# Attention of a hybrid layer with its scores turned: queries on the partitions instead of keys

## The chip, the cores and the metric

The kernel runs on one NeuronCore of a Trainium2 chip. The metric is device time in microseconds. TensorE multiplies (PE in the rows; PEld is its weight load, which runs beside it), VectorE (DVE), ScalarE (ACT) and GpSimd (POOL) do the element-wise work, and SyncE (SP) issues most transfers. Each engine takes its instructions strictly in the order of the built program; engines meet at semaphores.

## The reference, cut to what matters

One layer of a network over 512 latent tokens and 128 context tokens with 1024 features: modulated norm, one input projection that feeds an mLSTM (4 heads) and a latent attention (8 heads), an output projection over both, a residual, and an MLP. All of it is float32. The part that the change touches is the attention:

```python
def one(qi):
    s = jnp.einsum('bqhd,bkhd->bhqk', qi, kf) * scale
    p = jax.nn.softmax(s, axis=-1)
    return jnp.einsum('bhqk,bkhd->bqhd', p, vf)
```

For each of 8 heads, 512 latent queries attend to 640 keys (512 latent and 128 of the cached context), with 96 features in a query or key and 64 in a value. The 128 context tokens attend to their own 128 keys. The results of both go side by side into the rows 512 to 1023 of the operand of the output projection; the mLSTM's are rows 0 to 511.

## The kernel before

Tokens are kept as columns and features as partitions; a product that must be near float32 is taken as three products of parts: the high part `hi` (a cast to float32r on ScalarE) and the remainder `lo` (source less high part, on VectorE), as `hi*hi + hi*lo + lo*hi`. `split` (L108) makes the two. PSUM has two pools: `psD` has two tiles of two banks, `psS` four tiles of one bank. A helper `two` (L633) gives the 640 columns that lie in the two banks of a `psD` tile as 2 x 320.

The stage in question lies between the projections of queries and keys and the output projection. For each head, `head_q` and `head_k` (L911, L925) transpose the queries (`Tq`) and keys (`Tk`) to feature-major and split them. `row_max` (L934) multiplies the high parts with queries on partitions, four tiles of 640 columns, and takes the row maximum; `max_row` (L943) turns the four columns of maxima into one row, which rides as a 97th row of the contraction. `weights` (L971) takes for each of five blocks of 128 keys the scores with keys on the partitions, 512 query columns (`st`, L975 to L977), then the exponential, which ScalarE writes to SBUF, and its split `pu`; GpSimd adds the five blocks up into `tot` (L997) and makes one of the five remainders. `values` (L1000) multiplies the parts with the values into `pv`, adds the two halves, and writes 64 rows of `mix_a`. `sums` (L1016) takes the column sums of `tot` by products with ones; `normalise` (L1027) spreads the reciprocals of two heads over the partitions (`rdb`) and multiplies `mix_a`. `self_scores` and `self_out` (L950, L962) do the context's own queries (`cs`, `co`).

The loop at L1054 writes these steps in a pipelined order: the values follow the weights by two steps, the next head's preparation stands between the blocks of this one, and the normalisation follows by nine steps. The scheduler of the framework (`schedule_with_timeline_sim=True` at the launch) then chooses the order on each engine itself, from its own estimate of times, and the order in which a pool's tiles come free.

The output projection multiplies eight column blocks of weights by eight inputs: inputs 0 to 3 are the mLSTM's (`mh`, `ml` of `mix_m`), 4 to 7 are pairs of attention heads. `mmT` (L624) issues 6 products of 320 columns for each input. Its first two blocks, `wo0` and `wo4`, sit in both `psD` tiles; their inputs 0 to 3 are taken early, as work beside the last heads, inputs 4 to 7 after the last normalisation:

```python
with tc.issue_after(factors.ins):
    mmT(ps, w_first, MHv, MLv, KT, 4)
```

Then `gated` (L1109) adds the finished tile to the residual on VectorE (`xr`), which starts a long run of VectorE work up to the MLP.

## Time and profile before

| what | us |
|---|---|
| median of 3 runs | 898.63 |
| lowest and highest run | 898.08, 899.42 |
| span of the profiled execution | 896.7 |
| busy in the span: TensorE | 855.5 |
| VectorE | 637.7 |
| ScalarE | 407.6 |
| GpSimd | 341.7 |

The profile is of one execution on the one core; its own time is not listed apart, and its span, first instruction to last, is 1.9 us under the median of the runs. "Busy" counts the time that an engine had at least one instruction in work. TensorE's matmuls overlap and their ends are modelled, so its issue is read from the distance between starts. A row of the order of time has start, duration, engine, line, operation, output and inputs with shapes, and, in brackets, how long the engine was idle before and what released it. A row of a table by stretch has its two ends, its length, and the busy time (number of instructions) of each engine, then the granted TensorE clock as a share of full speed, the share of the transfer engines and GB/s. A row of grouped instructions has line, engine, operation, output and inputs, shapes and count, then the sum of busy time in us and the mean of one in ns, then idle time before them.

### The profile page before, as it was taken

The numbers are of one execution on the slowest core, as the hardware profiler recorded it, in microseconds if no ns is written. First come the engines' busy times: TensorE is split into PE (matmuls) and PEld (weight loads), VectorE is DVE, ScalarE is ACT, GpSimd is POOL, SyncE is SP. The second block draws the span as 40 slices with busy tenths as digits, with TensorE's granted clock in tenths as the row PEclk, the third lists the DMA queues.
The fourth block names the chain that finished last, engine by engine and source line by source line (L and its number), as shares of the span: only waits on it lengthen the run. The fifth ranks groups of instructions, "written<-read, shape, count | busy, mean of one in ns | idle before, by whom it ended". The sixth has DMA issues, their size and how long they took to land.

```text
span 896.7 us, 15205 instructions
## 1 busy us (share of the span) xinstructions
PE 855.5 (95%) x5775; PEld 797.9 (89%) x5775; DVE 637.7 (71%) x1276; ACT 407.6 (45%) x879; POOL 341.7 (38%) x343
## 2 busy tenths in 40 slices
PE   3999999999889999999979999999999999999998
PEld 2688789999768677799979999999999999999998
DVE  3754634546787789969989587695876949678673
ACT  3424426436864688844436143351434415244430
POOL 3100113313234567734745254352534427254320
PEclk9999999999999999999989999999999999999999
DMA  9742843231326100322130312122122221412122
GB/s 356 312 129 69 297 153 90 65 95 51 95 80 249 58 1 1 118 71 88 44 129 25 118 48 95 51 90 96 48 94 92 72 75 48 134 56 71 49 96 92
DMA packets 22329, 89.64 MB, mean 100 GB/s; under 512 B 3144, under 2 KB 3944, under 8 KB 18928
## 3 DMA queue, kind: packets, MB, share of 16 engines
q1 hardware_dynamic: 19440, 81.95, 26.5%
q0 software_dynamic: 1664, 4.26, 1.7%
q10 hardware_dynamic: 1152, 2.46, 0.7%
q8 instruction: 46, 0.75, 0.4%
q14 instruction: 27, 0.22, 0.1%
HBM read 85.33 MB, written 3.32 MB: 99 GB/s over the span
## 4 chain that ended last, share of the span: by engine, by line
PE 74%; DVE 16%; DMA 4%; issue 3%; ACT 3%; POOL 0%; SPq 0%; DVEq 0%; POOLq 0%; ACTq 0%
PE dn L630 23%; PE qk L630 6%; PE mo L630 3%; DMA st<-in_w_ada 3%; DVE wu L110 2%; PE pv L1006 2%; PE ada L389 2%; PE n L695 2%; PE up1M L1228 2%; PE wo L630 2%; DVE r L1272 1%; PE up8M L1228 1%; PE up10M L1228 1%; PE up14M L1228 1%; PE up15M L1228 1%
## 5 line engine op out<-in xcount | busy, mean ns | idle before, releaser
L1266 POOL TENSOR_TENSOR r<-r,rbs 128x320 f32<-128x320 f32 x64 | 77.3, 1222 | 120.7 <-DVE r L1244 118.8
L109 ACT CAST wh<-st 128x1024 fp32r<-128x1024 f32 (+4 forms) x69 | 69.4, 1008 | 105.2 <-PE dn L630 40.3
L1111 DVE SCALAR_TENSOR_TENSOR xr<-dn,modT,xr 128x320 f32<-128x320 f32 x64 | 35.2, 550 | 106.6 <-PE dn L630 106.6
L630 PE MATMUL dn<-fl,wh 128*128 128x320 f32 x448 | 103.6, 310 | 3.0 <-DVE fl L1273 3.0
L630 PE MATMUL dn<-fh,wh 128*128 128x320 f32 x448 | 103.0, 309 | 0.0
L630 PE MATMUL dn<-fh,wl 128*128 128x320 f32 x448 | 101.8, 309 | 0.0
L110 DVE TENSOR_TENSOR wl<-st,wh 128x1024 fp32r<-128x1024 f32 (+4 forms) x67 | 83.3, 1244 | 24.3 <-ACT wh L109 23.3
L109 ACT CAST wu<-S 128x512 fp32r<-128x512 f32 x64 | 37.6, 617 | 105.3 <-issue 46.7
L630 PEld LDWEIGHTS dn<-fl,wh 128*128 128x128 f32 x448 | 75.1, 188 | 4.6 <-DVE fl L1273 4.6
L630 PEld LDWEIGHTS dn<-fh,wh 128*128 128x128 f32 x448 | 75.3, 188 | 0.0
L630 PEld LDWEIGHTS dn<-fh,wl 128*128 128x128 f32 x448 | 74.9, 188 | 0.0
L1270 ACT ACTIVATE r<-r 128x192 f32<-128x192 f32 (+2 forms) x96 | 40.9, 464 | 41.0 <-DVE r L1244 27.3
L110 DVE TENSOR_TENSOR wu<-S,wu 128x512 fp32r<-128x512 f32 x64 | 55.6, 879 | 0.8 <-ACT wu L109 0.8
L722 POOL TENSOR_TENSOR W<-ngb,mask 128x128 f32<-128x128 f32 x40 | 19.3, 498 | 68.9 <-DVE p L732 30.9
L1272 DVE TENSOR_TENSOR r<-r 128x320 f32<-128x320 f32 x64 | 45.0, 721 | 0.2
L997 POOL TENSOR_TENSOR tot<-tot,p 128x512 f32<-128x512 f32 x24 | 37.2, 1549 | 5.9 <-ACT p L979 3.9
L219 POOL TENSOR_TENSOR S<-st,st 128x512 f32<-128x512 f32 x8 | 13.5, 1682 | 59.4 <-DVE wu L110 59.4
L109 ACT CAST wu<-pair 128x512 fp32r<-128x512 f32 x24 | 14.1, 615 | 47.4 <-PE dn L630 41.1
L110 DVE TENSOR_TENSOR pu<-p,pu 128x512 fp32r<-128x512 f32 x32 | 33.2, 1050 | 2.5 <-ACT pu L109 2.5
L1273 DVE TENSOR_TENSOR fl<-r,fh 128x320 fp32r<-128x320 f32 x56 | 32.4, 598 | 0.2
L1006 PE MATMUL pv<-pu,v 128*128 128x512 f32 x80 | 29.1, 426 | 2.3 <-DVE pu L110 2.0
L630 PE MATMUL wo<-mh,wh 128*128 128x320 f32 x128 | 29.6, 311 | 0.7 <-DVE xr L1113 0.7
(485 smaller groups left out, 2420.1 us busy)
## 6 DMA issues: line engine op xcount, KB each, us to landing
st<-in_w_ada SPq DMA_DIRECT2D x16, 1024.0 KB, 5.6
st<-in_w_down SPq DMA_DIRECT2D x32, 512.0 KB, 3.4
ad<-in_w_ada SPq DMA_DIRECT2D x8, 1024.0 KB, 16.7
st<-in_w_up SPq DMA_DIRECT2D x16, 512.0 KB, 3.8
pair<-in_w_up SPq DMA_DIRECT2D x16, 512.0 KB, 4.8
st<-in_w_qko SPq DMA_DIRECT2D x12, 512.0 KB, 3.6
st<-in_w_out SPq DMA_DIRECT2D x8, 512.0 KB, 3.4
x<-in_x SPq DMA_DIRECT2D x4, 640.0 KB, 7.0
```

The costliest lines, as they stand in the source:

```text
L109: S.copy(hi, src)
L110: return eng.tensor_tensor(out=lo, in0=src, in1=f(hi), op=ALU.subtract)
L630: PE.matmul(out[:, hf * 512:hf * 512 + HT], lhsT=wt[:, c], rhs=xt[k][:, hf * HT:(hf + 1) * HT], start=(k == 0 and xt is xh and wt is hi), ...
L722: G.tensor_tensor(out=W[:, dg:dg + P], in0=nb_[dr][:, j * P:(j + 1) * P], in1=mask[:, dr, :], op=ALU.add)
L997: G.tensor_tensor(out=tot[h], in0=first, in1=pj, op=ALU.add)
L1006: PE.matmul(pacc[h], lhsT=v_u[hf][:, j, hh_, :], rhs=w, start=j == 0 and k == 0, stop=j == 4 and k == 1)
L1111: V.scalar_tensor_tensor(out=xr[m][:, 0:HT], in0=ps[:, 0:HT], scalar=modT[:, gi_ + m, 0:1], in1=xr[m][:, 0:HT], op0=ALU.mult, op1=ALU.add)
L1228: PE.matmul(ps, lhsT=w[:, c], rhs=b[k], start=k == 0 and w is hi and b is bh, stop=k == 3 and w is lo)
L1266: G.tensor_tensor(out=t, in0=t, in1=rbs[:, c], op=ALU.mult)
L1270: S.activation(out=t[:, c0:c1], in_=t[:, c0:c1], func=AF.Relu, bias=r[n][:, w:w + 1])
L1272: V.tensor_tensor(out=t, in0=t, in1=t, op=ALU.mult)
L1273: V.tensor_tensor(out=FL[n][:, c], in0=t, in1=f(FH[n][:, c]), op=ALU.subtract)
```

## The change

Scores are now taken with queries on the partitions, all three parts, so that one tile of 128 queries by 640 keys (`sc`) gives its own row maximum; ScalarE's exponential takes that as bias and returns the row sum, VectorE takes its reciprocal, and GpSimd scales the row tile (`prow`, 128 x 640) in place. `turn` transposes the scaled weights on TensorE, a block of 128 keys at a time (`tp`), and splits from PSUM. `row_max`, `max_row`, the ones row, the addition `tot`, `sums` and `normalise` go. `Tq` moves from `psD` to `psS` and leaves the context's queries to `Tk`; two small copies `qc`, `kc` move from ScalarE to VectorE. In the loop the turns of a head follow its scores by five steps and the values by seven; seven of the eight inputs of the output projection are split inside the loop and come before the last wait, one after it. The diff, without the bodies of the functions that are dropped whole (they are above) and without two constants that only these used:

```diff
...
     mix_a = view(mix[1], 0, 4, T)
-    prep, negm, cden, punit, tot, pacc = {}, {}, {}, {}, {}, {}
+    prep, punit, pacc, prow = {}, {}, {}, {}
     def evac(ps, hi, lo, g):
...
         prep[h] += [u[:, 0:P], u[:, P:2 * P]]
-        qh, ql_, kh, kl_, qc, kc = prep[h]
-        G.memset(f(kh)[QK:QK + 1], 1.0)
-        pt = psD(f"Tq{h}")
-        for i in range(NT):
+        qh, ql_ = prep[h][0:2]
+        pt = psS(f"Tq{h}")
+        for i in range(4):
             PE.transpose(out=pt[0:QK, i * P:(i + 1) * P], in_=qn_u[hf][:, i, hh_, :], identity=ident)
         evac(pt[0:QK, 0:TL], qh[0:QK], ql_[0:QK], hgc[:, 0:1])
-        S.activation(out=qc[0:QK], in_=pt[0:QK, TL:T], func=AF.Copy, scale=hgc[:, 0:1])
     def head_k(h):
...
             PE.transpose(out=pt[0:QK, i * P:(i + 1) * P], in_=kn_u[hf][:, i, hh_, :], identity=ident)
+        PE.transpose(out=pt[0:QK, 6 * P:7 * P], in_=qn_u[hf][:, 4, hh_, :], identity=ident)
         evac(pt[0:QK, 0:T], kh[0:QK], kl_[0:QK], hgc[:, 1:2])
-        S.activation(out=kc[0:QK], in_=pt[0:QK, T:T + P], func=AF.Copy, scale=hgc[:, 1:2])
-    def row_max(h, i):
+        V.tensor_scalar(out=kc[0:QK], in0=pt[0:QK, T:T + P], scalar1=hgc[:, 1:2], scalar2=None, op0=ALU.mult)
+        V.tensor_scalar(out=qc[0:QK], in0=pt[0:QK, T + P:T + 2 * P], scalar1=hgc[:, 0:1], scalar2=None, op0=ALU.mult)
+    def soften(out, ps, axis, name):
+        nm, sr = sm("nm", [P, 1], bufs=3), sm("sr", [P, 1], bufs=3)
+        V.tensor_reduce(out=nm, in_=ps, axis=axis, op=ALU.max, negate=True)
+        e = S.activation(out=out, in_=ps, func=AF.Exp, bias=nm, accum_out=sr)
+        V.reciprocal(out=sr, in_=sr)
+        return e, sr
+    def scores(h, i):
         qh, ql_, kh, kl_, qc, kc = prep[h]
         if i == 0:
...
+            prow[h] = view(U2(php, f"p{h}"), 0, 4, T)
+        ps = psD(f"sc{h}{i}")
+        c = slice(i * P, (i + 1) * P)
+        for n_, (l_, r_) in enumerate(((qh, kh), (qh, kl_), (ql_, kh))):
+            for hf in range(2):
+                PE.matmul(ps[:, hf * 512:hf * 512 + HT], lhsT=l_[0:QK, c], rhs=r_[0:QK, hf * HT:(hf + 1) * HT], start=n_ == 0, stop=n_ == 2)
+        p_ = prow[h][:, i, :]
+        e, sr = soften(tw(p_), two(ps), AX.XY, f"{h}{i}")
+        G.tensor_scalar(out=p_, in0=p_, scalar1=sr, scalar2=None, op0=ALU.mult)
+        return e
     def self_scores(h):
...
         PE.matmul(ps, lhsT=qc[0:QK], rhs=kc[0:QK], start=True, stop=True)
...
         pc_ = view(wwp.tile([P, 512], F32, tag="W", name=f"pc{h}"), 0, 2, P)
-        S.activation(out=pc_[:, 0], in_=ps, func=AF.Exp, bias=mx, accum_out=cden[h])
+        e, sr = soften(pc_[:, 0], ps, AX.X, f"{h}c")
+        G.tensor_scalar(out=pc_[:, 0], in0=pc_[:, 0], scalar1=sr, scalar2=None, op0=ALU.mult)
         return pc_
...
         S.copy(mix_a[b:b + VD, h // 2, TL:T], ps[0:VD, P:2 * P])
...
+    def turn(h, j):
+        ps = psS(f"tp{h}{j}")
+        for i in range(4):
+            PE.transpose(out=ps[:, i * P:(i + 1) * P], in_=prow[h][:, i, j * P:(j + 1) * P], identity=ident)
+        if h < AH - 2:
+            pool, tag = ((whp, "wh"), (wlp, "wl"))[(5 * h + j) % 2]
             u = pool.tile([P, 1024], F32R, tag=tag, name=f"pu{h}{j}")
             hi, lo = u[:, 0:TL], u[:, TL:2 * TL]
...
         else:
...
+            hi, lo = (Tt(f"pu{h}{j}{k}", F32R, n=TL) for k in range(2))
+        split(hi, lo, ps)
+        punit[h, j] = hi, lo
     def values(h, j):
...
         for k, w in enumerate((hi, lo)):
-            PE.matmul(pacc[h], lhsT=v_u[hf][:, j, hh_, :], rhs=w, start=j == 0 and k == 0, stop=j == 4 and k == 1)
+            last = PE.matmul(pacc[h], lhsT=v_u[hf][:, j, hh_, :], rhs=w, start=j == 0 and k == 0, stop=j == 4 and k == 1)
         if j == 4:
...
             V.tensor_tensor(out=mix_a[b:b + VD, h // 2, 0:TL], in0=ps[0:VD], in1=tmp, op=ALU.add)
...
         return last
...
     head_k(0)
...
     pcs = {}
     mhu, mlu = [], []
...
+    MSP = ((4, 1), (4, 3), (5, 1), (5, 3), (6, 1), (6, 3), (7, 3))
+    DT, DV = 5, 7
+    for n in range(5 * AH + DV):
+        h, j = divmod(n, 5)
+        if h < AH:
+            if h == AH - 1 and j == 0:
                 wsplit(state["get"] + 3)
-            if (h, j) == (7, 4):
-                w_first = wget(("out", 0))
-                ps_first = psD("wo0")
-                mmT(ps_first, w_first, kview(mhu * 2), kview(mlu * 2), KT, 0, 4)
-            exp_, lo_ = weights(h, j)
+            if j < 4:
+                exp_ = scores(h, j)
             if (h, j) in MSP:
                 k = MSP.index((h, j))
-                if k == 0:
-                    mhu.append(U("mh0", F32R))
-                    mlu.append(U("ml0", F32R))
-                with tc.issue_after(exp_.ins), tc.issue_after(lo_.ins):
-                    split(view(mhu[0], k * T, T), view(mlu[0], k * T, T), mix_m[:, k, :])
...
+                if k % 4 == 0:
+                    mhu.append(U(f"mh{k // 4}", F32R))
+                    mlu.append(U(f"ml{k // 4}", F32R))
+                src = mix_m[:, k, :] if k < MH else mix_a[:, k - MH, :]
+                with tc.issue_after(exp_.ins):
+                    split(view(mhu[k // 4], (k % 4) * T, T), view(mlu[k // 4], (k % 4) * T, T), src)
+            if j == 1 and h + 1 < AH:
+                head_q(h + 1)
+            if j == 2 and h + 1 < AH:
+                head_k(h + 1)
             if j == 3:
+                pcs[h] = self_scores(h)
+            if j == 4:
                 self_out(h, pcs.pop(h))
...
+        if n == 5 * AH:
+            w_first = wget(("out", 0))
+            ps_first = psD("wo0")
+            mmT(ps_first, w_first, kview(mhu), kview(mlu), KT, 0, 7)
+        if 0 <= n - DT < 5 * AH:
+            turn(*divmod(n - DT, 5))
+        if 0 <= n - DV < 5 * AH:
+            factors = values(*divmod(n - DV, 5))
     MHv, MLv = kview(mhu), kview(mlu)
-    for k in range(4, KT):
-        split(MHv[k], MLv[k], mix_a[:, k % 4, :])
+    split(MHv[KT - 1], MLv[KT - 1], mix_a[:, KT - 1 - MH, :])
     xu2 = [U("xr0"), U("xr1")]
...
             with tc.issue_after(factors.ins):
-                mmT(ps, w_first, MHv, MLv, KT, 4)
+                mmT(ps, w_first, MHv, MLv, KT, 7)
         elif m == OUT_ORDER[1]:
...
             w = wnext(("out", m))
-            mmT(ps, w, MHv, MLv, KT, 0, 4)
+            mmT(ps, w, MHv, MLv, KT, 0, 7)
             with tc.issue_after(factors.ins):
-                mmT(ps, w, MHv, MLv, KT, 4)
+                mmT(ps, w, MHv, MLv, KT, 7)
         else:
```

*TensorE, heads 1 to 3.* In the names, the digits are head and block: `sc20` is the first score tile of head 2, `tp10` the first turned block of head 1. Before:

```order
L940 MATMUL mx30_3561<-qk3_3496 128x320 x2
L1020 MATMUL su1_3543<-ones_99,tot1_3392 128x2 x4
L940 MATMUL mx31_3565<-qk3_3496 128x320 x2
L975 MATMUL st22_3550<-qk2_3370 128x512
L976 MATMUL st22_3550<-qk2_3370 128x512
L977 MATMUL st22_3550<-qk2_3370 128x512
L940 MATMUL mx32_3582<-qk3_3496 128x320 x2
L1006 MATMUL pv2_3569<-pu20_3493,v0_2602 128x512
```

After:

```order
L946 MATMUL sc20_3443<-qk2_3342 128x320 x6
L990 MATMUL pv0_3392<-pu02_3389,v0_2598 128x512
L990 MATMUL pv0_3392<-pu03_3422,v0_2598 128x512
L946 MATMUL sc21_3466<-qk2_3342 128x320 x6
L990 MATMUL pv0_3392<-pu03_3422,v0_2598 128x512
L965 MATMUL co1_3427<-ident_94,pc1_3410 128x128
L974 MATMUL tp04_3432<-ident_94,p0_3219 128x128 x4
L974 MATMUL tp10_3456<-ident_94,p1_3307 128x128 x4
L967 MATMUL co1_3427<-pc1_3410,vctx_2596 64x128
L990 MATMUL pv0_3392<-pu04_3437,v0_2598 128x512
L946 MATMUL sc22_3501<-qk2_3342 128x320 x6
```

The scores of head 2 went from single-bank tiles, read by ScalarE alone, to double-bank tiles; the first turn of head 1 stands two score tiles behind that head's last one, and the third score tile of head 2 is behind that turn and behind `co1`.

*ScalarE, at the same place.* Before:

```order
L959 ACTIVATE pc2_3536,cd_3535<-cs2_3531,mx_3533 128x128
L109 CAST pu21_3516<-p21_3514 128x512
L979 ACTIVATE p22_3554<-st22_3550 128x512
L109 CAST pu22_3556<-p22_3554 128x512
L979 ACTIVATE p23_3576<-st23_3572 128x512
L966 COPY pc2_3536<-co2_3590 128x128
L109 CAST pu23_3578<-p23_3576 128x512
L979 ACTIVATE p24_3601<-st24_3597 128x512
```

After:

```order
L934 ACTIVATE p1_3307,sr_3403<-sc13_3395,nm_3402 128x640
L934 ACTIVATE pc1_3410,sr_3412<-cs1_3408,nm_3411 128x128
L966 COPY pc1_3410<-co1_3427 128x128
L109 CAST pu04_3437<-tp04_3432 128x512
L934 ACTIVATE p2_3442,sr_3451<-sc20_3443,nm_3450 128x640
L934 ACTIVATE p2_3442,sr_3474<-sc21_3466,nm_3473 128x640
L109 CAST pu10_3461<-tp10_3456 128x512
```

The exponential of a block was followed by its own cast; now two exponentials of the next head stand behind the copy of `co1`, whose weights GpSimd has scaled.

*TensorE, the end of the stage.* Before:

```order
L1020 MATMUL su7_4296<-ones_99,tot7_4188 128x2 x4
L1038 MATMUL rdb3_4303<-ident_94,rd_4207 64x128
L1038 MATMUL rdc3_4304<-ident_94,rd_4207 64x128 x2
L630 MATMUL wo0_4253<-mh1_4317,wh45_4157 128x320 x2
L630 MATMUL wo0_4253<-ml1_4318,wh45_4157 128x320 x2
L630 MATMUL wo0_4253<-mh1_4317,wl45_4158 128x320 x2
L1006 MATMUL pv7_4220<-pu72_4216,v1_2715 128x512
L630 MATMUL wo0_4253<-mh1_4317,wh45_4157 128x320 x2
L630 MATMUL wo0_4253<-ml1_4318,wh45_4157 128x320 x2
```

After:

```order
L990 MATMUL pv7_4387<-pu710_4369,v1_2711 128x512
L974 MATMUL tp73_4390<-ident_94,p7_4180 128x128 x4
L990 MATMUL pv7_4387<-pu711_4370,v1_2711 128x512
L990 MATMUL pv7_4387<-pu720_4383,v1_2711 128x512
L974 MATMUL tp74_4401<-ident_94,p7_4180 128x128 x4
L990 MATMUL pv7_4387<-pu721_4384,v1_2711 128x512
L990 MATMUL pv7_4387<-pu730_4395,v1_2711 128x512
L990 MATMUL pv7_4387<-pu731_4396,v1_2711 128x512
L990 MATMUL pv7_4387<-pu740_4406,v1_2711 128x512
L990 MATMUL pv7_4387<-pu741_4407,v1_2711 128x512
L628 MATMUL wo0_4310<-mh1_4057,wh45_4168 128x320 x2
L628 MATMUL wo4_4455<-mh1_4057,wh46_4172 128x320 x2
```

Before, projection products with inputs from the first six heads stand between the last sums, the last values and the factors; after, the two last turns and the value products of head 7 stand alone, behind all early products of `wo0` and `wo4`.

## Rows read from the trace of the kernel before

**Rows 1.** The chain that ended last: shares of the span by engine.

```profile
PE 74%; DVE 16%; DMA 4%; issue 3%; ACT 3%; POOL 0%; SPq 0%; DVEq 0%; POOLq 0%; ACTq 0%
```

**Rows 2.** Table by stretch, attention stage, with its heading; columns as told above.

```profile
core 0: us, PE busy (x) PEld busy (x) DVE busy (x) ACT busy (x) POOL busy (x), PEclk, DMA share, GB/s
297.00:312.80 15.80, 14.80 (x91) 11.77 (x88) 12.17 (x20) 12.04 (x26) 11.65 (x11) 1.00 0.01 2
312.80:323.30 10.50, 10.50 (x64) 8.61 (x63) 8.74 (x15) 9.51 (x22) 8.14 (x6) 1.00 0.00 1
...
335.00:347.50 12.50, 11.95 (x83) 9.41 (x82) 11.38 (x16) 9.21 (x20) 8.77 (x6) 1.00 0.00 0
...
394.70:404.40 9.70, 9.70 (x76) 9.11 (x76) 3.09 (x7) 1.69 (x3) 0.61 (x5) 1.00 0.00 0
```

**Rows 3.** Order of time, TensorE, with heads 6 and 7 in work.

```profile
384.85 0.95 PE L1020 MATMUL su<-ones,tot 128*128 128x2 f32 x8
385.67 0.48 PE L1006 MATMUL pv<-pu,v 128*128 128x512 f32 x1
385.99 0.40 PE L975 MATMUL st<-qk 97*128 97x512 f32 x1
...
386.69 0.46 PE L630 MATMUL wo<-mh,wl 128*128 128x320 f32 x2
386.99 0.46 PE L630 MATMUL wo<-mh,wh 128*128 128x320 f32 x2
```

**Rows 4.** Order of time, TensorE, transposes of 128 columns ahead of the stage.

```profile
264.46 0.77 PE L864 MATMUL qlt<-ident,ql_u 128*128 128x128 f32 x5
265.06 0.38 PE L781 MATMUL ht<-ident,hm 128*128 128x128 f32 x2
```

**Rows 5.** Groups of instructions by line and shape, 295 to 405 us.

```profile
L997 POOL TENSOR_TENSOR tot<-tot,p 128x512 f32<-128x512 f32 x24 | 37.2, 1549 | 5.9 <-ACT p L979 3.9 <-ACT mix L969 1.0
L110 DVE TENSOR_TENSOR pu<-p,pu 128x512 fp32r<-128x512 f32 x32 | 33.2, 1050 | 2.5 <-ACT pu L109 2.5
...
L941 DVE TENSOR_REDUCE nm<-mx 128x1 fp32r<-128x640 f32 x32 | 25.7, 814 | 1.8 <-PE mx L940 1.6
...
L979 ACT ACTIVATE p<-st 128x512 f32<-128x512 f32 x40 | 23.4, 596 | 6.6 <-PE st L977 5.5 <-PE cs L954 0.4
...
L909 DVE SCALAR_TENSOR_TENSOR qk<-Tk,small,qk 96x640 fp32r<-96x640 f32 x7 | 6.1, 872 | 3.2 <-ACT qk L908 3.2
...
L1012 DVE TENSOR_TENSOR mix<-pv,pvt 64x512 f32<-64x512 f32 x8 | 5.4, 676 | 1.7 <-ACT pvt L1010 1.6
...
L918 POOL MEMSET qk<- 1x640 f32 x6 | 3.8, 627 | 1.1 <-POOL tot L997 0.9
...
L1025 DVE RECIPROCAL rd<-cd 128x1 f32<-128x1 f32 x8 | 1.2, 149 | 0.1
```

**Rows 6.** Order of time, all engines, the end of the attention stage.

```profile
391.97 0.39 PE L977 MATMUL st<-qk 96*128 96x512 f32 x1
...
397.10 0.39 PE L1006 MATMUL pv<-pu,v 128*128 128x512 f32 x1
...
398.20 0.68 DVE L1012 TENSOR_TENSOR mix<-pv,pvt 64x512 f32<-64x512 f32 x1 [1.59 <-ACT pvt L1010]
...
400.79 0.73 ACT L109 CAST mh<-mix 128x640 fp32r<-128x640 f32 x1 [2.62 <-DVE mix L1041]
...
401.55 0.82 DVE L110 TENSOR_TENSOR ml<-mix,mh 128x640 fp32r<-128x640 f32 x1 [0.85 <-ACT mh L109]
...
404.32 0.55 DVE L1111 SCALAR_TENSOR_TENSOR xr<-wo,modT,xr 128x320 f32<-128x320 f32 x1 [1.95 <-PE wo L630]
```

**Rows 7.** Table by stretch, three places outside the stage, for the granted clock.

```profile
264.00:267.00 3.00, 2.36 (x19) 1.76 (x17) 2.61 (x8) 2.86 (x6) 0.00 (x0) 1.00 0.00 0
...
454.00:456.00 2.00, 0.03 (x1) 0.00 (x0) 2.00 (x3) 0.78 (x2) 2.00 (x5) 1.00 0.98 365
...
462.00:464.00 2.00, 2.00 (x10) 2.00 (x9) 1.52 (x4) 1.02 (x2) 0.00 (x0) 0.50 0.00 0
```

More of the change, by code (lines that the diff above doesn't have):

```diff
@@ L329, in hybrid_layer @@
     make_identity(nc, ident)
-    ones = const.tile([P, P], F32, name="ones")
-    V.memset(ones, 1.0)
     mean_col = const.tile([P, 2], F32, name="mean_col")
@@ L823, in hybrid_layer @@
     vctx = const.tile([P, 2, 4, VD], F32, name="vctx")
-    identr = sm("kc", [P, P], F32R)
-    V.tensor_copy(out=identr, in_=ident)
     for hf in range(2):
@@ L930, in head_k @@
             PE.transpose(out=pt[0:QK, i * P:(i + 1) * P], in_=kn_u[hf][:, i, hh_, :], identity=ident)
+        PE.transpose(out=pt[0:QK, 6 * P:7 * P], in_=qn_u[hf][:, 4, hh_, :], identity=ident)
         evac(pt[0:QK, 0:T], kh[0:QK], kl_[0:QK], hgc[:, 1:2])
-        S.activation(out=kc[0:QK], in_=pt[0:QK, T:T + P], func=AF.Copy, scale=hgc[:, 1:2])
-    def row_max(h, i):
+        V.tensor_scalar(out=kc[0:QK], in0=pt[0:QK, T:T + P], scalar1=hgc[:, 1:2], scalar2=None, op0=ALU.mult)
[7 more added lines that the diff above has]
+    def scores(h, i):
         qh, ql_, kh, kl_, qc, kc = prep[h]
         if i == 0:
-            negm[h] = sm("nm", [P, 4], F32R)
-        ps = psD(f"mx{h}{i}")
-        for hf in range(2):
-            PE.matmul(ps[:, hf * 512:hf * 512 + HT], lhsT=qh[0:QK, i * P:(i + 1) * P], rhs=kh[0:QK, hf * HT:(hf + 1) * HT], start=True, stop=True)
-        V.tensor_reduce(out=negm[h][:, i:i + 1], in_=two(ps), axis=AX.XY, op=ALU.max, negate=True)
-    def max_row(h):
-        nm = negm.pop(h)
-        ps = psS(f"mr{h}")
-        for i in range(4):
-            PE.matmul(ps[0:1, i * P:(i + 1) * P], lhsT=nm[:, i:i + 1], rhs=identr, start=True, stop=True)
-        S.copy(prep[h][0][QK:QK + 1], ps[0:1])
+            prow[h] = view(U2(php, f"p{h}"), 0, 4, T)
[8 more added lines that the diff above has]
+        return e
     def self_scores(h):
@@ L1012, in values @@
             V.tensor_tensor(out=mix_a[b:b + VD, h // 2, 0:TL], in0=ps[0:VD], in1=tmp, op=ALU.add)
-    rds, u2s = {}, {}
-    def sums(h):
-        ps = psS(f"su{h}")
-        t = tot.pop(h)
-        for i in range(4):
-            PE.matmul(ps[:, 2 * i:2 * i + 2], lhsT=t[:, i * P:(i + 1) * P], rhs=ones[:, 0:2], start=True, stop=True)
-        if h % 2 == 0:
-            rds[h // 2] = sm("rd", [P, NT, 2])
-        rd = rds[h // 2]
-        V.reciprocal(out=rd[:, 0:4, h % 2], in_=ps[:, 0:8].rearrange("p (a b) -> p a b", b=2)[:, :, 0])
-        V.reciprocal(out=rd[:, 4, h % 2:h % 2 + 1], in_=cden.pop(h))
-    def normalise(p):
-        rd = rds.pop(p)
-        if p < AH // 2 - 1:
-            pb = psD(f"rdb{p}")
-            parts = ((pb, 0, NT),)
-        else:
-            parts = ((psS(f"rdb{p}"), 0, 4), (psS(f"rdc{p}"), 4, NT))
-        for pb, i0, i1 in parts:
-            for i in range(i0, i1):
-                for k in range(2):
-                    last = PE.matmul(pb[VD * k:VD * k + VD, (i - i0) * P:(i - i0 + 1) * P], lhsT=rd[:, i, k:k + 1].broadcast_to([P, VD]),
-                              rhs=ident, start=True, stop=True, tile_position=(0, VD * k))
-            c = slice(i0 * P, i1 * P)
-            V.tensor_tensor(out=mix_a[:, p, c], in0=pb[:, 0:(i1 - i0) * P], in1=mix_a[:, p, c], op=ALU.mult)
         return last
@@ L1086, in hybrid_layer @@
+                src = mix_m[:, k, :] if k < MH else mix_a[:, k - MH, :]
[5 more added lines that the diff above has]
+                head_k(h + 1)
+            if j == 3:
                 pcs[h] = self_scores(h)
-            if j == 3:
+            if j == 4:
                 self_out(h, pcs.pop(h))
-        if 0 <= n - DV < len(steps):
-            values(*steps[n - DV])
@@ L1091, in hybrid_layer @@
-        if 0 <= n - DS < len(steps) and steps[n - DS][1] == 4:
-            sums(steps[n - DS][0])
-        if 0 <= n - DN < len(steps):
-            h, j = steps[n - DN]
-            if j == 4 and h % 2:
-                factors = normalise(h // 2)
-    mhu.append(U("mh1", F32R))
-    mlu.append(U("ml1", F32R))
+        if n == 5 * AH:
[4 more added lines that the diff above has]
+            turn(*divmod(n - DT, 5))
```

53 lines of the change are left out of this document (1 added, 52 removed).

## Prediction

> **What bounds the kernel now.** I read the chain of waits first, then the table of busy time by stretch, then the groups of instructions inside the attention stage, and last the order of time at its end. The chain lies on TensorE for 74% of the span and on VectorE for 16% [rows 1], so the question is how long TensorE needs for the stage and how long it stands still in it. The stage runs from 297.0 us, where the first stretch of [rows 2] begins, to 404.3 us, where VectorE takes up the first finished tile of the output projection [rows 6]: 107.3 us. Its first head takes 15.8 us, three undisturbed heads take 10.5, 11.7 and 12.5 us (first and last shown), and the last stretch 9.7 us [rows 2]. In those heads TensorE, VectorE and ScalarE are all busy over 73% and TensorE and VectorE over 83%: no engine stands out, and "busy" for TensorE is the modelled duration, not the pitch. So I count pitches.
>
> **TensorE's load by head.** From one start to the next, three 512-column products take 0.70 us, 0.233 each; two 320-column products take 0.30, 0.15 each; eight of the row-sum products take 0.82, 0.10 each [rows 3]; five transposes of 128 columns take 0.60, 0.12 each [rows 4]. Removed per head: 15 score products with keys on partitions (15 x 0.233 = 3.5), 8 for the row maximum (8 x 0.15 = 1.2), and `mr`, `su` and `rdb` (4 + 8 + 10 small ones, 2.2 at 0.10; that is an upper price, since some are shorter, and I take 1.9). Added: 24 score products with queries on partitions (24 x 0.15 = 3.6) and 20 transposes of weights (20 x 0.12 = 2.4). Unchanged: 10 value products (2.3), 11 transposes of q and k (1.3), the context's own (0.6). Sum before 10.8, after 10.2: 0.6 us saved a head, 5 us in all.
>
> **The other engines by head.** VectorE keeps four maxima of 0.81 and the two q and k remainders. Its four remainders of the weights cost 1.05 each with both inputs in SBUF while GpSimd adds up rows; now there are five, from PSUM, for which the nearest row is `mix<-pv,pvt`, 512 columns with one input in PSUM, 0.68 [rows 5]: 4.2 becomes 3.4. It gains five reciprocals for two and a half (0.15 each, +0.4), and two 128-column copies from ScalarE, which no row prices here: between a reciprocal's 0.15 and Tk's 0.87, I take 0.3 each, near a fifth of the latter. It loses the multiplication of the normalisation (0.4). Together 10.8 before, 10.6 after. ScalarE: five exponentials of 512 columns (0.60 each [rows 5]) become four of 640, scaled to 0.75 each, with a read of the accumulator; it loses the two copies and `mr`'s: about 0.6 less. GpSimd: four additions of 1.55, one remainder and one memset go; four row scalings of 640 columns and one of 128 come. No row shows such a scaling. The bounds are the memset of 640 columns, 0.63, and the two-input addition scaled from 512 to 640 columns, 1.94 [rows 5]; I take 1.2, between them since it reads one tensor and not two. That is 5 us a head against 8, under the other engines even at the upper bound; off the path by load, on it by order (below). A gain below nothing in any of these is excluded: each is work added to an in-order queue.
>
> [...]
>
> **Order, start and end.** Loads alone say five microseconds faster. Three places of the order say otherwise.
>
> *Start.* Before, the maximum needs only an eighth of a head's products and the exponentials run from the four single banks. After, a score tile stays in one of two double banks from its six products (0.9 us) through its maximum (0.81) to its exponential (0.75): 2.8 us with the hops, and `Tk` takes as long. Before head 0's turns can start, 8 of these fills pass, and until the last score tile of head 1 is read, 10. From 297.0 the first two need 0.7, then four and a half rounds; unqueued 2.8 each, but from the fourth on they queue behind turns on VectorE and ScalarE, so I take 3.5: 297.0 + 0.7 + 15.8 = 313.5. TensorE has some 9 us of work there and stands still for the rest.
>
> *Heads.* Then six more heads follow to the last score tile of head 7. The load says 10.2 each, and before, the measured heads lie 0.8 over their load (11.6 less 10.8). I take 10.6, half of that, since VectorE no longer stretches beside GpSimd. What holds it above the load is a loop that the order shows: the fourth score tile of a head, its maximum, exponential, reciprocal and scaling, then the next `tp` block, which on TensorE stands between the second and the third score tile of the following head; and ScalarE's copy of `co`, which waits for GpSimd and TensorE with two exponentials queued behind it. Six splits of `ml` inside the heads (0.82 each [rows 6]) and two of weights (1.3 each, scaled to 1024 columns) are 7.5 on VectorE; I count 5.5 and let the rest fall into its gaps. Last score tile: 313.5 + 63.6 + 5.5 = 382.6, its products 0.3 earlier at 382.3.
>
> *End.* Before, the last score product is issued at 391.97 and VectorE takes up the tile at 404.32 [rows 6], 12.3 us later, and TensorE has output-projection products to issue through the whole chain of sums, factors and splits. After, the lag of a head leaves 28 transposes (3.4), 13 value products (3.0), the context's own (0.6) and all 84 output-projection products of seven of eight inputs (12.6 at 0.15, 12.3 at the closer pitch of long runs) behind it: 19.3 us, in front of the last two turns. What then follows is a chain with next to nothing beside it, since both double banks are held: two turns and three value products 1.8, cast 0.62, remainder 0.68, then pv's issue to the end of `mix` 1.8 (397.10 to 398.88) and `mh` to the end of `ml` 1.6 (400.79 to 402.37) [rows 6], the last products 1.3, hops 0.1: 7.9. So 382.3 + 19.3 + 7.9 = 409.5 against 404.3: **5.2 us later**. From there both kernels issue the same projection in the same order, and I pass the shift on whole. The span becomes 901.9; the shown runs' median, 898.63, lies 1.9 over the profiled span of 896.7, so 903.8.
>
> The point from which the forecast turns: the last scores would have to issue by 377.1, that is 9.7 us a head, under TensorE's own load of 10.2, unless start or end is shorter than I make it.
>
> **Rivals.**
> *Loads win (faster).* If the two banks turn round unqueued at 2.8 us (313.5 becomes 310.3), heads run at their load (10.2, so 2.4 less) and the splits fall half into gaps (1.5 less), the stage ends 7.1 earlier than forecast: 1.9 us faster than before, 896.7; with an end chain 3 us of which turn out covered, 893.7. For it speaks that VectorE's contended remainders go; against it that the first head of before, with more banks to turn to, already takes 15.8 us [rows 2] for a load of 10.8. 22%. Half of that lands within 0.2% of before: 13%.
> *The scaling loop sets the period.* With GpSimd at its upper bound, 1.94, and every hop queued, the heads stay at 11.6 as before: six more microseconds, 909.8. It decides from about 1.5 us a scaling. The row of 12.5 shows that heads can be that long. 15%.
> *The clock falls at the end.* TensorE is near idle for some 7 us while the last head is finished. [...] 12%.
> [...]
>
> **How the numbers follow.** Forecast 903.8, 36%; loads win 22%; same 13%; slow loop 15%; clock at the end 12%; clock throughout 2%. A measurement of this kernel can tell about 0.2% (1.8 us) from no change. Faster by more: 0.22; within: 0.13; slower: 0.65. The range goes from 895.5, most of the way into the case of the loads, to 912, past the slow loop with the clock's part; it leaves out some 15%.
>
> **What would show it.** In the changed trace: VectorE's `pu` at 0.65 to 0.75; GpSimd's scaling between 0.63 and 1.94; TensorE's first `tp` near 308 and its wait there ended by VectorE or ScalarE; the starts of the heads' fourth score tiles 10 to 11.5 us apart; a gap of 5 us or more on TensorE between the last `wo4` filler and the last `wo0` products. Wrong if the last scores issue before 377, or if TensorE is covered through the last chain.

## The result and the profile after

The changed kernel takes 924.31 us (median of 4 runs, 921.56 to 930.15) against 898.36 (median of 4) for the kernel before beside it. The ratio on record is 1.031, 95% interval 1.0285 to 1.0334; the two medians alone give 1.029. It is slower, as forecast, but by 26 us and not by 5, and outside the range of 895.5 to 912. The profiled execution has a span of 923.1 us.

The page of the changed kernel: busy time and share of each engine, the granted clock by fortieths of the span (in tenths), and the chain that ended last.

```profile
PE 866.3 (94%) x5767; PEld 809.5 (88%) x5767; DVE 632.8 (69%) x1317; ACT 402.7 (44%) x879; POOL 345.5 (37%) x335
...
PEclk9999999999999889899998999999999999999999
...
PE 71%; DVE 16%; issue 5%; ACT 3%; DMA 3%; POOL 1%; SPq 0%; DVEq 0%; ACTq 0%
```

No engine is much busier than in the kernel before, and the chain looks like [rows 1]. The whole loss lies in the attention stage: VectorE takes up the first finished tile of the output projection (`xr`) at 431.5 us, 27.2 after the 404.3 of [rows 6], and from there both kernels need the same (923.1 less 431.5 is 491.6; 896.7 less 404.3 is 492.4).

The stage by heads, cut where VectorE takes the maximum of each head's `cs` (columns as in [rows 2]):

```profile
318.70:335.50 16.80, 13.90 (x70) 11.68 (x69) 9.39 (x20) 9.68 (x22) 8.09 (x5) 0.80 0.00 0
335.50:348.50 13.00, 11.96 (x75) 9.51 (x74) 9.67 (x22) 7.86 (x18) 8.09 (x5) 1.00 0.01 1
348.50:363.30 14.80, 12.02 (x75) 9.33 (x73) 10.90 (x24) 10.30 (x24) 8.09 (x5) 1.00 0.00 0
363.30:377.20 13.90, 11.39 (x69) 8.71 (x67) 10.45 (x23) 9.12 (x21) 9.03 (x5) 1.00 0.01 2
377.20:392.70 15.50, 13.70 (x70) 11.66 (x70) 10.95 (x24) 9.96 (x23) 8.58 (x5) 0.78 0.18 58
```

A head takes 13.0 to 16.8 us where [rows 2] showed 10.5 to 12.5, and in the three of full clock TensorE stands still for 1.0 to 2.8 us and each of the others for 3.3 or more. That looks like a loop between engines and not like a load. The groups of the stage (297 to 431.5 us; the last part is the engine's idle time before them and what ended it) say where it closes:

```profile
L949 POOL TENSOR_SCALAR p<-p,sr 128x640 f32<-128x640 f32 x32 | 62.9, 1972 | 40.4 <-DVE sr L935 40.3
...
L110 DVE TENSOR_TENSOR pu<-tp,pu 128x512 fp32r<-128x512 f32 x40 | 27.2, 683 | 25.8 <-ACT pu L109 25.7
...
L959 POOL TENSOR_SCALAR pc<-pc,sr 128x128 f32<-128x128 f32 x8 | 6.6, 825 | 0.6 <-DVE sr L935 0.6
...
L965 PE MATMUL co<-ident,pc 128*128 128x128 f32 x8 | 2.7, 332 | 8.8 <-POOL pc L959 8.8
...
L966 ACT COPY pc<-co 128x128 f32<-128x128 f32 x8 | 2.1, 265 | 21.3 <-PE co L965 21.3
```

ScalarE stands 21.3 us in front of one small copy, that of `co`; TensorE's `co` waits for GpSimd's scaling of the context's weights. One pass of the loop, in order of time, heads 3 and 4 (all engines, other rows left out):

```profile
347.76 0.81 DVE L933 TENSOR_REDUCE nm<-sc 128x1 f32<-128x640 f32 x1
...
348.67 0.79 ACT L934 ACTIVATE p<-sc,nm 128x640 f32<-128x640 f32 x1 [1.90 <-DVE nm L933]
...
350.02 0.15 DVE L935 RECIPROCAL sr<-sr 128x1 f32<-128x1 f32 x1
...
350.26 1.88 POOL L949 TENSOR_SCALAR p<-p,sr 128x640 f32<-128x640 f32 x1 [2.81 <-DVE sr L935]
...
352.13 0.60 POOL L959 TENSOR_SCALAR pc<-pc,sr 128x128 f32<-128x128 f32 x1
...
352.78 0.33 PE L965 MATMUL co<-ident,pc 128*128 128x128 f32 x1 [1.47 <-POOL pc L959]
...
352.95 1.04 PE L974 MATMUL tp<-ident,p 128*128 128x128 f32 x8
...
353.15 0.27 ACT L966 COPY pc<-co 128x128 f32<-128x128 f32 x1 [2.76 <-PE co L965]
353.58 0.58 ACT L109 CAST pu<-tp 128x512 fp32r<-128x512 f32 x1 [0.17 <-PE tp L974]
...
354.06 0.80 ACT L934 ACTIVATE p<-sc,nm 128x640 f32<-128x640 f32 x1
...
355.01 1.15 PE L946 MATMUL sc<-qk 96*128 96x320 f32 x6 [0.23 <-ACT p L934]
...
361.37 0.81 DVE L933 TENSOR_REDUCE nm<-sc 128x1 f32<-128x640 f32 x1
```

The fourth score tile's maximum starts at 347.76; its exponential, reciprocal and scaling follow; the context's weights queue behind that scaling on GpSimd (352.13), `co` behind them on TensorE, then the turns behind `co`, and on ScalarE the copy of `co` and the cast of the first turned block. Only then, at 354.06, may the next head's first exponential go, whose tile had its maximum from 349.29 on. It frees a score bank for the third tile (355.01), and the fourth comes to its maximum at 361.37. 6.3 us from maximum to exponential and 7.3 from there to the next fourth maximum make the 13.6 us of this head.

TensorE's clock falls as well, three times in the heads, each behind 2 us in which TensorE was busy for no more than 0.60, 0.56 and 0.27 (table by stretch, same columns, the first two):

```profile
322.00:324.00 2.00, 0.60 (x5) 0.60 (x6) 0.10 (x1) 0.24 (x1) 1.34 (x2) 1.00 0.00 0
...
326.00:328.00 2.00, 2.00 (x9) 1.91 (x9) 1.23 (x3) 1.08 (x4) 2.00 (x2) 0.50 0.01 4
...
380.00:382.00 2.00, 0.56 (x2) 0.24 (x2) 0.95 (x2) 0.00 (x0) 1.89 (x2) 1.00 0.02 4
...
384.00:386.00 2.00, 2.00 (x7) 1.87 (x8) 0.39 (x3) 2.00 (x6) 1.52 (x1) 0.50 0.00 0
```

TensorE is busy 0.6 of 2 us, and in the stretch after next the granted clock is 0.50. So there were three theories: **A**, the loop through GpSimd, `co` and ScalarE; **B**, the clock; **C**, the round of the two score banks by itself.

### The profile page after: what moved, and what is told of

It is laid out like the page before. It is cut to its first block, busy times and chain, and to the rows that moved or that the text cites. A ratio compares the mean times of both kernels' runs of the same rounds, so it can differ in the third digit from the quotient of the medians.

```text
span 923.1 us, 15227 instructions
## 1 busy us (share of the span) xinstructions
PE 866.3 (94%) x5767; PEld 809.5 (88%) x5767; DVE 632.8 (69%) x1317; ACT 402.7 (44%) x879; POOL 345.5 (37%) x335
## 4 chain that ended last, share of the span: by engine, by line
PE 71%; DVE 16%; issue 5%; ACT 3%; DMA 3%; POOL 1%; SPq 0%; DVEq 0%; ACTq 0%
PE dn L628 22%; PE qk L628 6%; PE wo L628 6%; DVE wu L110 3%; PE mo L628 3%; DVE r L1209 3%; PE sc L946 2%; PE ada L387 2%; PE n L693 2%; DVE r L1181 2%; PE tp L974 2%; PE up1M L1165 1%; DVE fl L1210 1%; PE up14M L1165 1%; PE up15M L1165 1%
## 5 line engine op out<-in xcount | busy, mean ns | idle before, releaser
L949 POOL TENSOR_SCALAR p<-p,sr 128x640 f32<-128x640 f32 x32 | 62.9, 1972 | 40.4 <-DVE sr L935 40.3
L946 PE MATMUL sc<-qk 96*128 96x320 f32 x192 | 39.4, 350 | 6.4 <-ACT p L934 5.5
L110 DVE TENSOR_TENSOR pu<-tp,pu 128x512 fp32r<-128x512 f32 x40 | 27.2, 683 | 25.8 <-ACT pu L109 25.7
L946 PEld LDWEIGHTS sc<-qk 96*128 96x128 f32 x192 | 33.4, 216 | 11.8 <-ACT p L934 9.0
L990 PE MATMUL pv<-pu,v 128*128 128x512 f32 x80 | 32.9, 461 | 1.8 <-DVE pu L110 1.7
## 6 DMA issues: line engine op xcount, KB each, us to landing
ad<-in_w_ada SPq DMA_DIRECT2D x8, 1024.0 KB, 16.8
```

The source lines that it names most:

```text
L110: return eng.tensor_tensor(out=lo, in0=src, in1=f(hi), op=ALU.subtract)
L946: PE.matmul(ps[:, hf * 512:hf * 512 + HT], lhsT=l_[0:QK, c], rhs=r_[0:QK, hf * HT:(hf + 1) * HT], start=n_ == 0, stop=n_ == 2)
L949: G.tensor_scalar(out=p_, in0=p_, scalar1=sr, scalar2=None, op0=ALU.mult)
L990: last = PE.matmul(pacc[h], lhsT=v_u[hf][:, j, hh_, :], rhs=w, start=j == 0 and k == 0, stop=j == 4 and k == 1)
```

## The experiments

Each kernel is compared with the kernel before on its own chip. "Less" is against the changed kernel's 1.0310, at 898 us. The right half is from each profile: the start of the maximum of head 1's fourth tile, from there to that of head 7, from there to `xr`, and `xr`. The forecast's row reads the prediction's 313.5 and 382.6 as the ends of these maxima, 0.81 us after their starts. The start differs between profiles of the same order by 1.3 to 2.5 us (the changed kernel and e10, e3 and e6, e7 and e8); their six heads agree to 0.1.

| kernel | ratio, 95% interval | less, us | start | six heads | end | xr |
|---|---|---|---|---|---|---|
| forecast | | | 312.7 | 69.1 | 27.7 | 409.5 |
| changed | 1.0310 (1.0285 to 1.0334) | | 317.3 | 87.2 | 26.9 | 431.5 |
| e1, context scaled on VectorE | 1.0197 (1.0161 to 1.0232) | 10 | 320.3 | 77.4 | 26.4 | 424.1 |
| e2, rows not scaled | 1.0139 (1.0105 to 1.0172) | 15 | 315.9 | 74.9 | 26.9 | 417.7 |
| e3, co later | 1.0062 (1.0042 to 1.0083) | 22 | 315.6 | 66.0 | 27.2 | 408.8 |
| e4, rows scaled on VectorE | 1.0240 (1.0209 to 1.0271) | 6 | 316.9 | 84.0 | 27.1 | 428.0 |
| e5, e3 with rows not scaled | 1.0018 (0.9998 to 1.0038) | 26 | 315.7 | 65.7 | 24.6 | 405.9 |
| e6, e3 with wo4 held | 1.0033 (1.0015 to 1.0050) | 25 | 316.8 | 66.1 | 24.9 | 407.8 |
| e7, co in two halves | 1.0128 (1.0092 to 1.0165) | 16 | 316.5 | 67.8 | 28.7 | 413.0 |
| e8, e7 with wo4 held | 1.0073 (1.0047 to 1.0099) | 21 | 314.1 | 67.9 | 24.5 | 406.4 |
| e9, gap filled | 1.0285 (1.0255 to 1.0315) | 2 | 316.6 | 82.9 | 28.1 | 427.6 |
| e10, wo4 held, co in place | 1.0270 (1.0242 to 1.0298) | 4 | 318.6 | 87.2 | 24.0 | 429.8 |
| e11, e6 and e1 | 1.0053 (1.0033 to 1.0073) | 23 | 318.6 | 68.1 | 24.6 | 411.3 |
| e12, copy of co on VectorE | 1.0239 (1.0187 to 1.0292) | 6 | 321.7 | 84.9 | 28.4 | 435.0 |

**e1: one link of the loop shortened.** TensorE's order in the heads is unchanged.

```diff
-        G.tensor_scalar(out=pc_[:, 0], in0=pc_[:, 0], scalar1=sr, scalar2=None, op0=ALU.mult)
+        V.tensor_scalar(out=pc_[:, 0], in0=pc_[:, 0], scalar1=sr, scalar2=None, op0=ALU.mult)
```

> The edit moves one multiplication a head, that of the context's own weights, from GpSimd to VectorE; the order on TensorE stays as in the changed kernel. Theory A (scaling loop): in the changed kernel this multiplication (0.60 us) stands on GpSimd behind the scaling of the fourth row tile (1.88 us), the co transpose waits for it on TensorE, and ScalarE's copy of co waits for that with two exponentials behind it; so co comes 1.6 us earlier a head and the time falls by 11 us (7 heads), to 911 to 915. Theory B (clock): the low-clock stretches cost the most; the gaps shrink, the clock rises from 0.979, 4 to 6 us less. Theory C (two score banks turn round too slowly by themselves, scaling or not): under 3 us less, 921 or more.

Measured: 10 us less, near A's 11 in sum; the six heads lose 9.8, while the start in its profile is 3 later. But the 1.6 us a head that A gave are not there. From fourth tile to fourth tile the changed kernel takes 15.5, 14.9, 13.6, 14.5, 15.5 and 13.2 us, at a granted clock of 0.78, 1.00, 1.00, 1.00, 0.78 and 0.87; e1 takes 13.1, 12.7, 13.1, 14.0, 14.2 and 10.4, all at 1.00. In the third and fourth of these the shorter link gives 0.5 us each. The other 8.8 came in the second head (2.2) and in the three where the clock had been low, in the last of which GpSimd's 0.60 us had also taken 2.40 (last section). The third in e1, where the changed kernel has 347.76, 354.06 and 361.37 (all engines, other rows left out):

```profile
346.09 0.81 DVE L933 TENSOR_REDUCE nm<-sc 128x1 f32<-128x640 f32 x1
...
351.89 0.80 ACT L934 ACTIVATE p<-sc,nm 128x640 f32<-128x640 f32 x1
...
359.19 0.81 DVE L933 TENSOR_REDUCE nm<-sc 128x1 f32<-128x640 f32 x1
```

From maximum to exponential it is 5.8 us and not 6.3; the rest is 7.3 as before. The shorter link shortens just that part of the loop that A names. C alone is out: the two banks are as they were, and yet the pass is shorter.

**e2: another link taken out.** `scores` without the scaling of `p_`, so that the image tokens' result is not normalised.

> The scaling of the row tiles is left out (so the turned weights and the attention output of the image tokens are not normalised); the context's own weights are still scaled on GpSimd; TensorE's order is that of the changed kernel. Theory A: GpSimd is empty when the reciprocal of the context's row comes, co moves up by 1.3 us a head, and the turns no longer wait for GpSimd: 10 to 14 us less, 910 to 914, heads near 12.2 us. Theory C: heads stay at 13.2 to 15.5 us and the time at 920 or more. If the time falls below 905, scaling explains nearly all of the loss against the kernel before.

Measured: 15 us less, a head of 12.5. The same pass of the loop, with the clock at 1.00:

```profile
342.45 0.81 DVE L933 TENSOR_REDUCE nm<-sc 128x1 f32<-128x640 f32 x1
...
347.64 0.80 ACT L934 ACTIVATE p<-sc,nm 128x640 f32<-128x640 f32 x1
...
354.95 0.81 DVE L933 TENSOR_REDUCE nm<-sc 128x1 f32<-128x640 f32 x1
```

That is 5.2 and again 7.3: the 1.88 us of scaling are worth 1.1 in this head, because `co` then waits for the context's own reciprocal and its 0.60 us. GpSimd's scaling explains about half of the loss, not nearly all: with nothing on GpSimd but the context's 0.60 us, heads still are 1.5 us longer than in e3.

**e3: the loop opened.** In the program the context's output is written three score tiles later; what GpSimd does is untouched.

```diff
-            if j == 4:
-                self_out(h, pcs.pop(h))
+            if j == 2 and h:
+                self_out(h - 1, pcs.pop(h - 1))
...
         if n == 5 * AH:
+            self_out(AH - 1, pcs.pop(AH - 1))
```

> The context's own output (co, its copy, its product) is issued three score tiles later, behind the following head's third score tile; nothing else is changed and GpSimd still scales all rows. Theory A: neither TensorE nor ScalarE stands still at co any more, and the first turn that needs the fourth scaled row tile is all that is left of the loop: 2 to 2.5 us a head, 14 to 17 us less, 907 to 910, granted clock 0.99 or more. Theory C: 920 or more. Theory B: the clock rises, yet only 4 to 6 us come back.

Measured: 22 us less, more than any theory gave it, and 0.42 to 0.83% slower than the kernel before. The six heads fall from 87.2 to 66.0. The groups of e3 (297 to 409 us):

```profile
L949 POOL TENSOR_SCALAR p<-p,sr 128x640 f32<-128x640 f32 x32 | 62.5, 1961 | 18.0 <-DVE sr L935 17.6
...
L965 PE MATMUL co<-ident,pc 128*128 128x128 f32 x8 | 2.3, 283 | 1.1 <-DVE qk L905 1.0
L966 ACT COPY pc<-co 128x128 f32<-128x128 f32 x8 | 2.1, 260 | 3.2 <-PE co L965 3.2
L969 ACT COPY mix<-co 64x128 f32<-64x128 f32 x8 | 2.1, 260 | 8.0 <-PE co L967 8.0
```

GpSimd scales at the same 1.96 us a tile; the waits at `co` (8.8 on TensorE, 21.3 on ScalarE) are down to 1.1 and 3.2; a part is back as 8.0 in front of the copy of the product (L969, 2.0 in the changed kernel). So the place of this one step in the order is worth 22 us. It is not shown that all of it is the wait at `co`: the scheduler laid the rest anew around the moved step (the first `tp` comes at 305.2 us and not at 311.3, and one turned block stands right behind `co` where there were two), and no run holds that order fixed.

**e5: is the scaling still a cost?** e3 and e2 together.

> The context's own output is issued three score tiles later, as in e3_co_later, and on top of it the scaling of the row tiles is left out (so the attention output of the image tokens is not normalised). Theory A1 (the loop ran through GpSimd only by way of co): with co out of the way the scaling hides in the lag of a head, and leaving it out gives 0 to 3 us against e3_co_later: 900 to 903. Theory A2 (GpSimd's 1.9 us a tile is a cost of its own on the turns): as much as between the changed kernel and e2_no_rows, 14 us: 889.

Measured: 4 us less than e3, just over A1's 0 to 3. With `co` in place the same scaling was worth 15, so it mattered by way of `co`; a rest of some 4 us is its own, of which the profiles show 2.6 at the end (24.6 against 27.2), where the last head has no lag to hide it in.

**e4: the scaling moved, not removed.** `G.tensor_scalar` of the rows becomes `V.tensor_scalar`.

> The four row scalings a head go from GpSimd to VectorE, the context's stays on GpSimd. The nearest row is a VectorE multiplication of 512 columns by a column of factors, 0.48 us, so 0.6 each and 2.4 a head on VectorE, whose load becomes 13 us a head. Theory A: the latency of scaling falls by 1.3 us and by the queue ahead of the context's, 1.5 to 2 us a head less, unless VectorE's load takes it back: 908 to 918. Theory C, where VectorE's maxima are in the loop: slower than the changed kernel, 925 to 932.

Measured: 919.8 us, just outside A's 908 to 918. A VectorE scaling took 0.557 us, so the latency fell as thought, yet the six heads still take 84.0: 18 us more work on VectorE took back most of it.

**e9: the clock by itself.** Five products of the unit matrix ahead of each `co`, with the turns held behind it by an order constraint. In the trace the products stand a score tile ahead of `co`, and the heads have the changed kernel's order; at the start the first turns come earlier.

```diff
-        PE.transpose(out=ps[:, 0:P], in_=pc_[:, 0], identity=ident)
+        for _ in range(5):
+            PE.matmul(ps[:, 2 * P:3 * P], lhsT=ident, rhs=ident, start=True, stop=True)
+        cot[h] = PE.transpose(out=ps[:, 0:P], in_=pc_[:, 0], identity=ident)
...
-            turn(*divmod(n - DT, 5))
+            hc, jc = divmod(n, 5)
+            if jc == 4 and hc < AH:
+                with tc.issue_after(cot[hc].ins):
+                    turn(*divmod(n - DT, 5))
+            else:
+                turn(*divmod(n - DT, 5))
```

> The changed kernel with its order kept, and five products of the unit matrix with itself, whose result nobody reads, ahead of each co transpose on TensorE, where it waits for GpSimd: TensorE is busy for some 1.4 us more a head in a stretch where it stood still. Theory A (loop through GpSimd, co and ScalarE sets the time, the clock only follows): the granted clock rises from 0.979 to 0.985 or more, and the heads stay at 13 to 15 us where the clock was full anyway; the two heads of 15.5 to 16.8 lose some 2 us each, 3 to 6 us less in all: 918 to 921. Theory B (the clock is the main cause): the clock goes to 0.99 and 10 to 15 us come back: 909 to 914. Rival: the added products cost more than the clock gives, 925 to 930.

Measured: 2 us less, where A had 3 to 6, and the intervals of the two ratios overlap. The heads in its table by stretch:

```profile
317.30:331.10 13.80, 11.84 (x81) 10.03 (x80) 9.16 (x21) 8.38 (x20) 8.10 (x5) 1.00 0.00 1
331.10:344.80 13.70, 12.50 (x83) 10.20 (x81) 9.75 (x22) 8.54 (x20) 8.10 (x5) 1.00 0.01 1
...
373.50:388.20 14.70, 12.62 (x80) 10.23 (x80) 10.92 (x24) 9.89 (x23) 9.02 (x5) 1.00 0.29 103
```

The clock is full in every head, 0.992 over the span against 0.979, and the heads still take 13.7 to 14.7 us. The two of low clock shown above (16.8 and 15.5) do shrink, to 13.8 and 14.7, while the pass of the loop from 347.76 takes 13.6 us in both kernels. The clock follows the gaps and adds to them, by 4 us in the six heads of these two profiles; with it full they still take 82.9 against the forecast's 69.1, so B is not the main cause.

**e10 and e6: the end.** The seven-input products of `wo4` are held back until the last turn is issued (`tlast[7, 4]`), in the changed kernel (e10) and in e3 (e6).

```diff
-            mmT(ps, w, MHv, MLv, KT, 0, 7)
+            with tc.issue_after(tlast[7, 4].ins):
+                mmT(ps, w, MHv, MLv, KT, 0, 7)
```

> The changed kernel with co where it is, and only the products of wo4 held back until the last turn has been issued, as in e6_late_hold. If start, heads and end add up as separate terms, the same 2 to 5 us come off here: 919 to 922, and the first finished tile comes some 2 us sooner after the last score product. If the end only gave in e6_late_hold because VectorE was the limit there, nothing: 924.

> As e3_co_later, and the products of the second output-projection tile (wo4) are held back until the last turn of the last head has been issued, so that they stand beside the last remainders, the copy of pv and the last split. In e3_co_later TensorE stands still for 3 us before the last wo0 products and its granted clock falls to 0.50 right behind. Theory (the end is a chain without cover): the first finished tile comes 3 us earlier and the clock stays at 1.00, 4 to 5 us less than e3_co_later: 898 to 899, within 0.3% of the kernel before. Rival (the end is bound by TensorE's 84 products and 28 transposes as a sum, or by VectorE): under 1.5 us less.

Measured: 4 us less in the changed kernel, 3 less than e3; e6's 3 lie between its two expectations. Both pairs of intervals overlap, so the size is not settled, but both profiles show the end shorter by 2.9 and 2.3 us. In e3 (order of time, then the table by stretch):

```profile
403.32 1.55 PE L990 MATMUL pv<-pu,v 128*128 128x512 f32 x6
...
407.01 0.85 PE L628 MATMUL wo<-mh,wh 128*128 128x320 f32 x4 [2.15 <-ACT mh L109]
```

```profile
404.00:408.00 4.00, 1.85 (x9) 1.10 (x8) 1.51 (x2) 1.31 (x2) 0.53 (x5) 1.00 0.00 0
408.00:412.00 4.00, 3.75 (x15) 3.38 (x16) 3.24 (x7) 3.32 (x4) 0.13 (x1) 0.57 0.00 0
```

and the same places in e6:

```profile
403.00:407.00 4.00, 4.00 (x28) 3.87 (x26) 1.51 (x2) 1.31 (x2) 0.32 (x3) 1.00 0.00 0
407.00:411.00 4.00, 3.26 (x22) 3.03 (x22) 3.18 (x7) 3.29 (x4) 0.10 (x1) 1.00 0.00 0
```

In e6 TensorE is covered through the last chain, and the clock stays up behind it.

**e7, e8, e11: three tries at more.** In e7 transposition and copy of `co` go with the third tile, product and copy out two steps later; e8 adds the held `wo4`; e11 is e6 with e1's edit.

> The context's output in two halves: transposition and copy with the following head's third tile, product and copy out two steps later. In e3_co_later ScalarE still waits 8.0 us in all for the product with exponentials behind it. If these waits are on the path, 0.7 us a head come back, 5 us: 897 to 899. If VectorE's load (near 1.8 of each 2 us busy in these heads) now sets the pace, under 2 us: 901 to 903.

> e6_late_hold and e7_two_halves together. If both edits give what they promise, 893 to 895, faster than the kernel before by 0.3 to 0.6%; if only the end gives, 898 to 900; if neither, 902.

> e6_late_hold with the multiplication of the context's weights on VectorE, as in e1_pc_vec: GpSimd has 0.6 us a head less in its queue ahead of the row tiles, and its one stretch of 2.6 us beside VectorE's remainders of a weight tile goes. If GpSimd's queue is what e5_late_no_rows gave back 4 us of, 1 to 2 us: 898 to 899.5, not told from the kernel before. If VectorE's load decides, 0 to 2 us more: 900.5 to 902.5.

None pays. e7 is 6 us slower than e3, against both expectations: its heads are 1.8 us longer and its end 1.5; which order made it so was not followed up. e8 is not told from e3, e11 not from e6. No version beat the kernel before: e6 is 0.15 to 0.50% slower, and e5, which leaves work out, is at best equal.

**e12: which of the two queues holds?** The copy of `co` goes to VectorE.

> The changed kernel with the copy of co moved from ScalarE to VectorE; the orders of TensorE, of GpSimd and of the rest of ScalarE stay. Theory S (the copy is what holds ScalarE's exponentials back): the exponentials of the next two score tiles no longer stand behind it, about 1 us a head, 7 to 10 us less, 914 to 917. Theory T (TensorE's in-order wait at co holds everything behind it, and the next cast of a turned block, which follows co on TensorE, stands on ScalarE ahead of the same exponentials anyway): 0 to 3 us less, 921 to 924. Rival: the copy now holds up VectorE's maxima, some us more.

The time is inconclusive: the runs range from 917.8 to 929.5, and the interval touches the changed kernel's. The profile says more, though it is of the 929.5. The three heads that have the full clock in both take 14.95, 13.67 and 14.52 us against 14.89, 13.61 and 14.47: nothing is gained. The same pass of the loop:

```profile
352.18 0.81 DVE L933 TENSOR_REDUCE nm<-sc 128x1 f32<-128x640 f32 x1
...
358.06 0.59 ACT L109 CAST pu<-tp 128x512 fp32r<-128x512 f32 x1 [3.25 <-PE tp L974]
...
358.54 0.80 ACT L934 ACTIVATE p<-sc,nm 128x640 f32<-128x640 f32 x1
```

With the copy gone to VectorE, ScalarE stands in front of the next cast, whose turned block is behind `co` on TensorE, and the exponential again starts 6.4 us after the maximum. In these heads TensorE's queue holds by itself, as theory T has it; whether the copy alone would hold too is not shown.

## Why the prediction was right and wrong

- **The direction: right.** Order and not load decides. VectorE's load did go down as priced (the remainders of the weights take 0.683 us from PSUM, priced 0.68; [rows 5] had 1.05), and it did not help. The two small copies were priced 0.3 each as near a fifth of 0.87, which is 0.17; they took 0.34.
- **The start: 4.7 us short.** The round of two banks was priced 3.5 us for four and a half rounds. Head 1's last tile came at 317.3, and the first `tp` at 311.3 and not near 308. The prediction's terms are of full clock; in the changed kernel the three stretches of 2 us from 308 to 314 are all like this one:

```profile
308.00:310.00 2.00, 2.00 (x8) 2.00 (x9) 0.43 (x2) 0.82 (x3) 2.00 (x2) 0.50 0.03 8
```

In e3 the clock is 1.00 there and the tile comes at 315.6; in e6, with the same order, it is 0.50 from 300 to 308 and the tile comes at 316.8; from the first tile's maximum on that is 16.7 us in e3 and 19.5 in e6, and 18.0 in the changed kernel. So part of the 4.7 is the clock; how much was the first `co` is not shown.
- **The heads: the step that failed.** "I take 10.6, half of that, since VectorE no longer stretches beside GpSimd." 69.1 us for six heads, measured 87.2; with the start's 4.7 and an end 0.8 shorter that makes the 22 us by which `xr` is late. The prediction names the loop in the very next sentence, `co`'s copy with two exponentials behind it included, and prices it at 0.4 us a head, half of what the old heads exceeded their load by, though the old loop had other links. The links were at hand: maximum 0.81, exponential 0.75, reciprocal 0.15, a scaling of 1.94 and a fifth of one for the context; that is 4 us, with `co`, the copy and the hops still to come, in which the next head's exponentials may not start. Measured it is 6.3 of the 13.6 us at full clock. The other 7.3, from that exponential to the next fourth tile, no row of before gave. Some 4 of the 18 us are the clock that fell behind the gaps (e9). In e3, with this loop open, the six heads take 66.0 and the stage ends at 408.8, 0.7 from the 409.5 forecast; that is luck, a start 2.9 later against heads 3.1 and an end 0.5 shorter.
- **The rival of the slow loop: right mechanism, wrong price.** It held the heads at 11.6 because the old ones were; nothing tied the new loop to that number. Its threshold, 1.5 us a scaling, was passed by 1.88. It got 15% and 909.8; it should have been summed as a chain.
- **GpSimd's price.** 1.2 us was taken "since it reads one tensor and not two". Measured 1.88 undisturbed, 1.97 in the mean: 2.94 ns an element (1.88 over 640) against 3.03 for the two-input addition of [rows 5] (1.549 over 512). The second input had cost next to nothing, 0.09 ns, so the upper bound was the right row. The three scalings that stand back to back take 5.60 us, so the price is not a matter of how one is recorded.
- **The end: right in sum**, 26.9 against 27.7. From the last filler, which ends at 423.8, to the last `wo0` products it is 5.6 us, but TensorE stands still for only 2.2 of them, since the two last turns and seven value products lie between; the clock fell behind that, as the rival of 12% had it:

```profile
429.44 0.85 PE L628 MATMUL wo<-mh,wh 128*128 128x320 f32 x4 [2.15 <-ACT mh L109]
```

```profile
431.00:435.00 4.00, 3.75 (x17) 3.38 (x17) 3.53 (x8) 2.81 (x4) 0.00 (x0) 0.61 0.05 8
```

The range to 912 holds a part for this clock that no run shows by itself. What the runs showed in its place: in e6 the clock is 1.00 from 407 to 411, where e3 has 0.57 from 408 to 412, and the end is 2.3 us shorter, the cover of TensorE included.
- **Loads win: not even with the loop open.** e5, with no scaling and no `co` in the way, is not faster than the kernel before (0.9998 to 1.0038), and its stage ends at 405.9 against the 404.3 of [rows 6].
- **The clock throughout: wrong cause.** It did fall inside the heads, to 0.78 in two of them, but behind gaps, and e9's heads, with as many transposes, run at 1.00, as do the transposes from 264 to 267 us in [rows 7]; in this mix no run shows them to lower the clock.
